# The upper weight sum of the projections' seven-product pairs, made by an adding transfer of GpSimd's queue instead of a VectorE addition

## The chip, the core and the metric

The kernel runs on one core of one Trainium2 chip. The metric is the device time of one execution in microseconds (us). Every run lists the time of the whole execution; the profiler adds the span from the first to the last instruction of one profiled execution. Engines are named as the profile names them: PE (TensorE matmuls), ACT (ScalarE), DVE (VectorE), POOL (GpSimd) and SP (SyncE, which here only issues transfers). An engine works through its instructions in the order in which they stand in its queue, and an instruction that waits holds back all that stand behind it on that engine.

## The reference

Two layers, each a mixer and a feed-forward part, on 256 tokens of 2048 columns in float32.

```python
for l in range(DEPTH):
    h = rms_norm(x, pre_mix_norm[l])
    m = hybrid_mixer(h, l, w_in[l], w_o[l], ...)      # h @ w_in, two kinds of attention, mix @ w_o
    x = x + rms_norm(m, post_mix_norm[l])
    h = rms_norm(x, pre_ffn_norm[l])
    f = swiglu(h, w_gate[l], w_up[l], w_down[l])      # (silu(h @ w_gate) * (h @ w_up)) @ w_down
    x = x + rms_norm(f, post_ffn_norm[l])
```

The change concerns the two projections of the mixer: `h @ w_in` (2048 to 6144 columns; its columns are the q, k and v of eight stick-breaking heads and of eight differential heads) and `mix @ w_o` (2048 to 2048).

## The kernel before

**Weights.** All weights are cut into blocks of 256 rows (two groups of 128 partitions) by 512 columns, 512 KB each, and laid out in the order of their use: 784 blocks, 392 a layer. `weight_order` makes the order; the number in a tile's name (`GU21`, `hi21`) is the block's place in it. A block `i` is loaded by SP (`fetch`, L258), then split into a rounded part `hi` (ACT) and a rest `lo` (DVE), both in float32r, and a product is three matmuls: left-hi by hi, left-hi by lo, left-lo by hi (`product`, L1225 to L1227). Weight blocks are prepared four ahead of the one in use (`LOOKAHEAD`), and the `hi` and `lo` tiles have six buffers each.

**Seven-product pairs.** Two weight blocks of the same rows and two column groups, g (block i-1) and u (block i), with the two token halves, make a two-by-two block product. Some of these pairs are done with seven products in place of eight. They need sums of weight blocks, which `mixed_weights(i)` makes from the loaded tiles g and u, whose halves `[:, 0, :]` and `[:, 1, :]` are the upper and the lower 128 rows:

- T1 = upper g + upper u, written over upper u. This is the sum that the change moves. `split(hi, lo, u)` then splits T1 and lower u together (ACT L307, DVE L309).
- T2 = lower u - T1 (DVE L318), then split into the third part of `Th`, `Tl`.
- g + T2 (DVE L319, both halves), which gives T3 and T4, then split into the first two parts of `Th`, `Tl`.

The matmuls of a pair (`seven_products`) come in this order: upper g (`hi`, `lo` of block i-1), lower g, T1, lower u, T2, T3, T4.

**Which pairs.** In the feed-forward part 122 pairs (`sevens`) have their own way: `summed` loads u into a tile T up to four blocks early and GpSimd's queue adds upper g onto it straight from the weights in memory (L275, `accum_op=ALU.add`). In the input projection there are ten pairs a layer and in the output projection four (`plain`, `own`): 28 in all. Their u is loaded like other blocks, into a tile GU (`late_room`, four buffers) or V (two buffers), and T1 is made by DVE at L313.

**The input projection around the change.** The columns are taken in six pairs of column groups (`PAIRS`). The first pair, (6, 8), has no seven-product pairs. When its sums are complete, `settle` scales them (ACT L1055, tiles `tok`), and `rotate` turns the first quarter of each head dimension by four small operations on POOL for each of four tiles (L914 to L917). Meanwhile the second column pair, (10, 7), starts; its third weight pair, blocks 20 and 21, is the first seven-product pair of the layer, blocks 24 and 25 the second. In layer 1 the same places are blocks 412, 413 and 416, 417. Each of the first column pairs is followed by the attention work of finished heads, which is spread between the matmuls.

**What sets the order.** The program is recorded in the order of the code, and a scheduler with its own estimates of durations then sets each engine's queue; `issue_after` puts one instruction behind another (`after_rests()` puts L313 behind the newest plain rest on DVE; `not_ahead` keeps a load of a pair behind earlier loads on SP), and `high_priority` moves work ahead. An instruction waits for the ones whose data it needs.

Of the kernel before, what the change touches and what calls it, by code (L numbers as in the profile page):

```python
# [13 lines left out]
ALU = mybir.AluOpType  # L14
# [170 lines left out]
def kernel(  # L185
# [15 lines left out]
    nc = tc.nc  # L201
# [19 lines left out]
    order, plan, sevens, plain, own, aside = weight_order()  # L221
    stream = [weights_in_turn[i].rearrange("p (k n) -> p k n", k=2) for i in range(len(order))]
# [12 lines left out]
    def fetch(upto):  # L235
        while len(raws) < min(upto, len(stream)):
            i = len(raws)
            for j in range(i, min(i + EARLY + 1, mix_raw[3])):
                if j in sevens and j not in sums:
                    summed(j)  # L240
            if i in sevens:
                raws.append(sums[i])
                continue
            if i + 1 in sevens:
                g = mix_raw[0].tile([P, 2, CW], F32, tag="G", bufs=mix_raw[1], name=f"G{i}")
                with not_ahead(i):
                    loads.append(nc.sync.dma_start(g, stream[i]))
                raws.append(g)
                continue
            if i in own or i + 1 in own:  # L250
                raw = mix_pool[0].tile([P, 2, CW], F32, tag="v", bufs=2, name=f"V{i}")
            elif i in plain or i + 1 in plain:
                raw = late_room([P, 2, CW], f"GU{i}")
            else:
                raw = wpool.tile([P, 2, CW], F32, tag="raw", bufs=4, name=f"raw{i}")
            mixing = bool({i, i + 1} & (own | plain))
            with not_ahead(i) if mixing else nullcontext():
                loads.append(nc.sync.dma_start(raw, stream[i]))  # L258
            raws.append(raw)
            if not mixing:  # L260
                usual.append((i, loads[-1]))

    usual = []

    def not_ahead(i):

        return tc.issue_after(next(load.ins for j, load in reversed(usual) if j <= i - LEAD))

    sums = {}
    def summed(i):  # L270

        sums[i] = mix_raw[0].tile([P, 2, CW], F32, tag="T", bufs=mix_raw[2], name=f"T{i}")
        with not_ahead(i):
            loads.append(nc.sync.dma_start(sums[i], stream[i]))
        nc.gpsimd.dma_start(sums[i][:, 0, :], stream[i - 1][:, 0, :], accum_op=ALU.add)  # L275
# [5 lines left out]
    def mixed_weights(i):  # L281

        g, u = raws[i - 1], raws[i]
        hi = wpool.tile([P, 2, CW], F32R, tag="hi", bufs=6, name=f"hi{i}")
        lo = wpool.tile([P, 2, CW], F32R, tag="lo", bufs=6, name=f"lo{i}")
        if i in own or i in aside:
            th = wpool.tile([P, 2, CW], F32R, tag="hi", bufs=6, name=f"Th{i}")
            tl = wpool.tile([P, 2, CW], F32R, tag="lo", bufs=6, name=f"Tl{i}")
        if i in own:
            th2 = mix_pool[0].tile([P, 2 * (S + P)], F32R, tag="ah", bufs=1, name=f"T2h{i}")[:, 0:CW]  # L290
            tl2 = mix_pool[0].tile([P, 2 * (S + P)], F32R, tag="al", bufs=1, name=f"T2l{i}")[:, 0:CW]
        elif i in aside:
            if aside[i] == "v":
                both = heads_pool[0].tile([P, 2, CW], F32R, tag="v", bufs=2, name=f"T2{i}")
                th2, tl2 = both[:, 0, :], both[:, 1, :]
            else:
                th2, tl2 = (
                    mix_pool[0].tile([P, 4, P], F32R, tag=tag, bufs=len(IN_SEVEN), name=f"T2{tag}{i}").rearrange("p j c -> p (j c)")
                    for tag in ("sh", "sl")
                )  # L300
        else:
            th = mix_pool[0].tile([P, 3, CW], F32R, tag="Th", bufs=1 if i in plain else 2, name=f"Th{i}")
            tl = mix_pool[0].tile([P, 3, CW], F32R, tag="Tl", bufs=1 if i in plain else 2, name=f"Tl{i}")
            th2, tl2 = th[:, 2, :], tl[:, 2, :]

        def split(h, l, w):
            nc.scalar.activation(h, w, AF.Copy)  # L307
            with in_row(i):
                newest_rest[i] = nc.vector.tensor_tensor(out=l, in0=w, in1=h.bitcast(F32), op=ALU.subtract)  # L309

        if i in plain or i in own:
            with after_rests():
                nc.vector.tensor_tensor(out=u[:, 0, :], in0=g[:, 0, :], in1=u[:, 0, :], op=ALU.add)  # L313
        split(hi, lo, u)
        t1, b22 = ((hi[:, k, :], lo[:, k, :]) for k in range(2))
        t3, t4 = ((th[:, k, :], tl[:, k, :]) for k in range(2))
        t2 = u[:, 1, :]
        nc.vector.tensor_tensor(out=t2, in0=t2, in1=u[:, 0, :], op=ALU.subtract)  # L318
        nc.vector.tensor_tensor(out=g, in0=g, in1=t2.unsqueeze(1).to_broadcast([P, 2, CW]), op=ALU.add)  # L319
        split(th2, tl2, t2)  # L320
        split(th[:, 0:2, :], tl[:, 0:2, :], g)
        t2 = th2, tl2
        return {"b22": b22, "t1": t1, "t2": t2, "t3": t3, "t4": t4}

    def feed(upto):
        fetch(upto)
        while fed[0] < min(upto, len(stream)):
            i = fed[0]
            raw = raws[i]
            if i in sevens or i in plain or i in own:  # L330
                ready[i] = mixed_weights(i)
                fed[0] += 1
                continue
            hi = wpool.tile([P, 2, CW], F32R, tag="hi", bufs=6, name=f"hi{i}")
            nc.scalar.activation(hi, raw, AF.Copy)  # L335
            lo = wpool.tile([P, 2, CW], F32R, tag="lo", bufs=6, name=f"lo{i}")
            if i in helped:
                rest = nc.gpsimd.tensor_tensor(out=lo, in0=raw, in1=hi.bitcast(F32), op=ALU.subtract)
                if helped[i]:
                    tc.add_manual_dep(rest.ins, newest_seven[0].ins.name, AFTER, reason="the shared port")  # L340
                ready[i] = (hi, lo)
                fed[0] += 1
                continue
            with behind():
                rest = nc.vector.tensor_tensor(out=lo, in0=raw, in1=hi.bitcast(F32), op=ALU.subtract)  # L345
            ready[i] = (hi, lo)
            fed[0] += 1
            rests.append(rest)

    def rounded_next():  # L350

        i = fed[0]
        fetch(i + 1)
        raw = raws[i]
        hi = wpool.tile([P, 2, CW], F32R, tag="hi", bufs=6, name=f"hi{i}")
        nc.scalar.activation(hi, raw, AF.Copy)
        lo = wpool.tile([P, 2, CW], F32R, tag="lo", bufs=6, name=f"lo{i}")
        ready[i] = (hi, lo)
        fed[0] += 1

        def rest(eng=nc.vector):
            r = eng.tensor_tensor(out=lo, in0=raw, in1=hi.bitcast(F32), op=ALU.subtract)
            if eng is nc.vector:
                rests.append(r)
            return r

        return rest
# [5 lines left out]
    def in_row(i):  # L373

        return tc.issue_after(follows[i].ins) if i in follows else nullcontext()
# [8 lines left out]
    def after_rests():  # L384

        return tc.issue_after(rests[-1].ins)
# [39 lines left out]
    def late_room(shape, name, dtype=F32):  # L426

        return rooms.tile(shape, dtype, tag="late", name=name)
# [490 lines left out]
    def opening(pool, accs, xT, stats, sums_of, settle):  # L919
# [33 lines left out]
        for kk in range(2):  # L953
            for i in range(2):
                loads.append(nc.sync.dma_start(raws[i][:, kk, :], stream[i][:, kk, :]))
        load()
        fetch(4)
        for kk in range(2):
            split(kk)
# [407 lines left out]
    for l in range(L):  # L1367
# [42 lines left out]
        for kp in LATE_O[:-1]:  # L1410
            i, j = (plan[l]["o"][c, kp] for c in (2, 3))
# [97 lines left out]
        for c in range(FF // CW):  # L1509
# [47 lines left out]
            for t in range(NT):  # L1557
                nc.vector.scalar_tensor_tensor(
                    out=results[c][t], in0=banks[2 * t + 1], scalar=rs[t][:, 0:1], in1=w[2 * t], op0=ALU.mult, op1=ALU.mult
# [197 lines left out]
```

## Time and profile before

| what | value |
|---|---|
| three runs | 2177.02 us median, 2175.26 to 2178.78 |
| the profiled execution's own time | 2176.12 us |
| its span, first to last instruction | 2174.4 us, TensorE clock granted 0.999 |
| ACT busy | 1415.4 us (65%) |
| POOL busy | 246.4 us (11%) |
| transfers | 470.44 MB, mean 216 GB/s |
| GpSimd's queue | 17600 packets, 32.02 MB, 8.9% of 16 transfer engines' span |

Matmuls are pipelined, so PE's busy time says only that it always has one under way; where it waits is read from the view of waits. A row of the timeline has the start and the duration in us, the engine, the source line, the operation and its output and inputs without their numbers, the shapes, a count, and in brackets the idle time of the engine before it and what ended that.

### The profile page before, as it was taken

The page shows a single profiled execution, that of the slowest core. Times are in us where ns is not written, and L with a number is a line of the kernel's source. Part 1 is how long each engine was busy: PE and PEld are TensorE (multiplying, and loading weights), DVE is VectorE, ACT ScalarE, POOL GpSimd, SP SyncE. Part 2 cuts the span into 40 slices and gives each one's busy share as a digit, 9 for nine tenths or more (in the row PEclk, how much of TensorE's full clock was granted, in tenths as well). Part 3 has the DMA queues.
Part 4 walks back from the last instruction along what each step waited for, and adds up shares of the span by engine and source line. Part 5 has one row for each costly group of instructions (what it writes and reads, how often), then busy time and mean ns, then how long its engine had stood idle before and what let it go on. Part 6 is the DMA issues. An engine that isn't in the chain of part 4 may idle for free.

```text
span 2174.4 us, 28786 instructions
## 1 busy us (share of the span) xinstructions
PE 2162.2 (99%) x9932; PEld 1778.7 (82%) x9932; DVE 1959.8 (90%) x2705; ACT 1415.4 (65%) x2113; POOL 246.4 (11%) x239
## 2 busy tenths in 40 slices
PE   9999999999999999999999999999999999999998
PEld 7888888888888888888888888888888888888886
DVE  7888978899999999999878888779999999999997
ACT  7666775765666666666575667757566666676664
POOL 1100000022221220000010000000212222200000
PEclk9999999999999999999999999999999999999999
DMA  8545446497887876768465464455978878767683
GB/s 315 204 165 196 161 174 204 153 306 233 246 259 224 230 236 225 235 224 257 146 245 175 171 206 161 172 182 183 302 232 253 254 224 243 226 220 241 202 270 98
DMA packets 140275, 470.44 MB, mean 216 GB/s; under 512 B 15952, under 2 KB 16976, under 8 KB 139616
## 3 DMA queue, kind: packets, MB, share of 16 engines
q1 hardware_dynamic: 121952, 436.03, 58.3%
q0 software_dynamic: 17600, 32.02, 8.9%
q8 instruction: 78, 1.28, 0.2%
q10 hardware_dynamic: 576, 0.54, 0.1%
q14 instruction: 69, 0.57, 0.1%
HBM read 460.14 MB, written 8.39 MB: 215 GB/s over the span
## 4 chain that ended last, share of the span: by engine, by line
PE 90%; DVE 5%; issue 2%; ACT 1%; DMA 1%; DVEq 0%; ACTq 0%
PE c L1282 20%; PE in L1225 6%; PE in L1227 6%; PE in L1226 6%; PE dn L1608 4%; PE dn L1605 4%; PE dn L1606 4%; PE p L1226 3%; PE c L1225 2%; PE c L1227 2%; PE p L1227 2%; PE c L1226 2%; PE p L1225 2%; PE o L636 2%; PE o L634 2%; PE o L635 2%
## 5 line engine op out<-in xcount | busy, mean ns | idle before, releaser
L345 DVE TENSOR_TENSOR lo<-raw,hi 128x1024 fp32r<-128x1024 f32 x442 | 535.4, 1231 | 54.6 <-ACT hi L335 53.5
L335 ACT ACTIVATE hi<-raw 128x1024 fp32r<-128x1024 f32 x464 | 473.6, 1054 | 69.2 <-DMA raw<-in_weights_in_turn_dram 25.4
L1282 PE MATMUL c<-hi,xF 128*128 128x512 f32 x1344 | 364.5, 392 | 0.6 <-DVE xF L544 0.5
L1282 PEld LDWEIGHTS c<-hi,xF 128*128 128x128 f32 x1344 | 249.8, 188 | 53.3 <-ACT act L1492 1.7
L275 POOL DMA_DIRECT2D T<-in_weights_in_turn_dram x122 | 107.3, 879 | 1363.7 <-DVE f L1499 557.3
L1282 PE MATMUL c<-lo,xF 128*128 128x512 f32 x672 | 207.4, 390 | 0.0
L307 ACT ACTIVATE Th<-T 128x512 fp32r<-128x512 f32 x122 | 77.2, 633 | 196.6 <-DVE T L318 194.2
L307 ACT ACTIVATE Th<-G 128x1024 fp32r<-128x1024 f32 x122 | 129.1, 1058 | 79.3 <-DVE G L319 78.4
L1605 PE MATMUL dn<-hi,jh 128*128 128x512 f32 x416 | 162.0, 389 | 0.0
L1606 PE MATMUL dn<-lo,jh 128*128 128x512 f32 x416 | 161.8, 389 | 0.0
L309 DVE TENSOR_TENSOR Tl<-G,Th 128x1024 fp32r<-128x1024 f32 x122 | 149.1, 1222 | 11.6 <-ACT Th L307 11.6
L335 ACT ACTIVATE hi<-G 128x1024 fp32r<-128x1024 f32 x122 | 128.9, 1057 | 36.6 <-DMA G<-in_weights_in_turn_dram 18.4
L309 DVE TENSOR_TENSOR lo<-T,hi 128x1024 fp32r<-128x1024 f32 x122 | 151.3, 1240 | 0.1
L319 DVE TENSOR_TENSOR G<-G,T 128x1024 f32<-128x1024 f32 x122 | 148.9, 1221 | 2.6 <-DVE T L318 0.9
L1282 PEld LDWEIGHTS c<-lo,xF 128*128 128x128 f32 x672 | 126.0, 188 | 26.5
L345 DVE TENSOR_TENSOR lo<-G,hi 128x1024 fp32r<-128x1024 f32 x104 | 127.0, 1221 | 10.1 <-ACT hi L335 10.0
L307 ACT ACTIVATE hi<-T 128x1024 fp32r<-128x1024 f32 x122 | 128.1, 1050 | 11.5 <-PE c L1227 8.0
L1608 PE MATMUL dn<-hi,jl 128*128 128x512 f32 x416 | 128.1, 389 | 0.0
L1225 PE MATMUL in<-hi,xT 128*128 128x512 f32 x316 | 126.0, 400 | 0.4 <-ACT hi L961 0.4
L1226 PE MATMUL in<-lo,xT 128*128 128x512 f32 x316 | 123.3, 391 | 0.3 <-DVE lo L345 0.2
L1227 PE MATMUL in<-hi,xT 128*128 128x512 f32 x316 | 123.1, 391 | 0.0
L1225 PE MATMUL in<-hi,xI 128*128 128x512 f32 x292 | 117.1, 401 | 0.0
(532 smaller groups left out, 5049.4 us busy)
## 6 DMA issues: line engine op xcount, KB each, us to landing
raw<-in_weights_in_turn_dram SPq DMA_DIRECT2D x482, 512.0 KB, 4.8
T<-in_weights_in_turn_dram SPq DMA_DIRECT2D x122, 512.0 KB, 5.2
G<-in_weights_in_turn_dram SPq DMA_DIRECT2D x122, 512.0 KB, 5.4
T<-in_weights_in_turn_dram POOLq DMA_DIRECT2D x122, 256.0 KB, 5.6
GU<-in_weights_in_turn_dram SPq DMA_DIRECT2D x48, 512.0 KB, 6.2
V<-in_weights_in_turn_dram SPq DMA_DIRECT2D x8, 512.0 KB, 5.6
away_ffn<-x SPq DMA_DIRECT2D x8, 512.0 KB, 7.5
xd<-away_ffn SPq DMA_DIRECT2D x8, 512.0 KB, 9.0
```

Of the source, the lines that this page charges most:

```text
L307: nc.scalar.activation(h, w, AF.Copy)
L309: newest_rest[i] = nc.vector.tensor_tensor(out=l, in0=w, in1=h.bitcast(F32), op=ALU.subtract)
L319: nc.vector.tensor_tensor(out=g, in0=g, in1=t2.unsqueeze(1).to_broadcast([P, 2, CW]), op=ALU.add)
L335: nc.scalar.activation(hi, raw, AF.Copy)
L345: rest = nc.vector.tensor_tensor(out=lo, in0=raw, in1=hi.bitcast(F32), op=ALU.subtract)
L1225: nc.tensor.matmul(a, sh, hi, start=first, stop=False, skip_group_check=open_sums[0])
L1226: nc.tensor.matmul(a, sh, lo, start=False, stop=False, skip_group_check=open_sums[0])
L1227: return nc.tensor.matmul(a, sl, hi, start=False, stop=last, skip_group_check=open_sums[0])
L1282: nc.tensor.matmul(a, stat[part], w[j][:, kk, :], start=first and kk + n == 0, stop=last and kk == 1 and n == 2)
L1605: nc.tensor.matmul(accs[c, t], sh, hi[:, kk, :], start=first, stop=False, skip_group_check=open_sums[0])
L1606: nc.tensor.matmul(accs[c, t], sh, lo[:, kk, :], start=False, stop=False, skip_group_check=open_sums[0])
L1608: nc.tensor.matmul(accs[c, t], sl, hi[:, kk, :], start=False, stop=last, skip_group_check=open_sums[0])
```

## The change

The addition at L313 is taken out of `mixed_weights`. In `fetch`, right behind the load of a block u of the 28 pairs, GpSimd's queue gets a transfer that adds upper g, read from the weights in memory, onto upper u in its tile. The numbers are the same; the transfer waits for the load of u to land.

```diff
@@ fetch @@
             if not mixing:
                 usual.append((i, loads[-1]))
+            elif i in own or i in plain:
+                nc.gpsimd.dma_start(raw[:, 0, :], stream[i - 1][:, 0, :], accum_op=ALU.add)
@@ mixed_weights @@
-        if i in plain or i in own:
-            with after_rests():
-                nc.vector.tensor_tensor(out=u[:, 0, :], in0=g[:, 0, :], in1=u[:, 0, :], op=ALU.add)
         split(hi, lo, u)
```

The scheduler also places other instructions anew. Three places follow; the line numbers of the changed kernel are two higher below the first edit and one lower behind the second.

POOL of the changed kernel in layer 0, between the rotation of the last of the four tiles of column pair (6, 8) (`tok0_8_1`) and the first rotation of the next column pair (`tok0_7_0`):

```order
L913 TENSOR_TENSOR ra_0_8_1_582<-tok0_8_1_580,rope_sb_95 128x128
L914 TENSOR_TENSOR rb_0_8_1_583<-tok0_8_1_580,rope_sb_95 128x8x8
L915 TENSOR_TENSOR rb_0_8_1_583<-tok0_8_1_580,rope_sb_95 128x8x8
L916 TENSOR_TENSOR tok0_8_1_580<-ra_0_8_1_582,rb_0_8_1_583 128x8x16
L263 DMA GU21_622<-in_weights_in_turn_dram 128x512
L263 DMA GU25_712<-in_weights_in_turn_dram 128x512
L263 DMA GU37_1024<-in_weights_in_turn_dram 128x512
L263 DMA GU41_1146<-in_weights_in_turn_dram 128x512
L913 TENSOR_TENSOR ra_0_7_0_979<-tok0_7_0_977,rope_sb_95 128x128
```

Before, `ra_0_7_0` stood directly behind `tok0_8_1`; the four adding transfers are new, and the first stands behind all sixteen operations of the four rotations.

DVE in layer 0 around block 21 (`Tl21` first from T2, then from T3 and T4 together). Before:

```order
L345 TENSOR_TENSOR lo20_620<-GU20_600,hi20_618 128x1024
L313 TENSOR_TENSOR GU21_622<-GU20_600,GU21_622 128x512
L309 TENSOR_TENSOR lo21_625<-GU21_622,hi21_624 128x1024
L318 TENSOR_TENSOR GU21_622<-GU21_622 128x512
L345 TENSOR_TENSOR lo22_670<-raw22_666,hi22_668 128x1024
L319 TENSOR_TENSOR GU20_600<-GU20_600,GU21_622 128x1024
L309 TENSOR_TENSOR Tl21_627<-GU21_622,Th21_626 128x512
L345 TENSOR_TENSOR lo23_676<-raw23_672,hi23_674 128x1024
L309 TENSOR_TENSOR Tl21_627<-GU20_600,Th21_626 128x1024
```

and with the change:

```order
L344 TENSOR_TENSOR lo20_620<-GU20_600,hi20_618 128x1024
L311 TENSOR_TENSOR lo21_626<-GU21_622,hi21_625 128x1024
L344 TENSOR_TENSOR lo22_670<-raw22_666,hi22_668 128x1024
L317 TENSOR_TENSOR GU21_622<-GU21_622 128x512
L344 TENSOR_TENSOR lo23_676<-raw23_672,hi23_674 128x1024
L318 TENSOR_TENSOR GU20_600<-GU20_600,GU21_622 128x1024
L311 TENSOR_TENSOR Tl21_628<-GU21_622,Th21_627 128x512
L311 TENSOR_TENSOR Tl21_628<-GU20_600,Th21_627 128x1024
```

The addition is gone, and `lo22` and `lo23` now stand ahead of the steps that lead to T3 and T4. On ACT `hi21` stands directly behind `hi20` in both kernels, with `hi22` and `hi23` behind it.

POOL of the changed kernel in layer 1, at the same place of the program:

```order
L263 DMA GU413_10501<-in_weights_in_turn_dram 128x512
L913 TENSOR_TENSOR ra_1_6_0_10449<-tok1_6_0_10447,rope_sb_95 128x128
...
L916 TENSOR_TENSOR tok1_8_1_10483<-ra_1_8_1_10485,rb_1_8_1_10486 128x8x16
L263 DMA GU417_10586<-in_weights_in_turn_dram 128x512
L263 DMA GU429_10883<-in_weights_in_turn_dram 128x512
```

Here the first transfer (block 413) stands ahead of the four rotations, and the second (block 417) behind them.

## The prediction

> **What bounds the kernel now.** I read the busy times first, then the chain of waits, then what PE waited for in the two stretches where the change acts: the input and output projection with the attention, 40 to 385 us (layer 0) and 1105 to 1460 us (layer 1).
>
> ```profile
> PE 2162.2 (99%) x9932; PEld 1778.7 (82%) x9932; DVE 1959.8 (90%) x2705; ACT 1415.4 (65%) x2113; POOL 246.4 (11%) x239
> PE 90%; DVE 5%; issue 2%; ACT 1%; DMA 1%; DVEq 0%; ACTq 0%
> ```
>
> PE is 90% of the chain that ends last. The only wait of PE that the view lists in the two stretches is one in each, layer 0 first:
>
> ```profile
> PE pT_df L895 <- DVE w L1268: 0.2, 1, 0.2
> ```
> ```profile
> PE pT_df L895 <- DVE w L1268: 0.5, 1, 0.5
> ```
>
> So PE's stream sets the time here. Work taken off DVE can win back at most 0.2 + 0.5 = 0.7 us; anything that makes PE wait adds in full, since PE, busy for 99% of the span, has no idle time later in which to make it up.
>
> **What is removed.** The two groups of additions, and what ACT's idle time says of them:
>
> ```profile
> L313 DVE TENSOR_TENSOR GU<-GU,GU x24: 670/686/954, 53.9 to 1377.2; 128x512 f32<-128x512 f32 x24
> L313 DVE TENSOR_TENSOR V<-V,V x4: 681/685/686, 342.8 to 1441.5; 128x512 f32<-128x512 f32 x4
>   DVE GU L313: 27.9, 15
> ```
>
> 28 x 0.69 = 19.2 us of DVE time, and 27.9 us in which ACT stood idle for the sum before it could split u. Both lie beside PE's matmuls, so they are worth nothing by themselves. I take the 0.7 us of PE's two waits as won, because both are waits for DVE and two additions stand ahead of each; the other bound is 0.
>
> **What is added.** 28 adding transfers of 256 KB. The kernel has the same transfer 122 times in the feed-forward part:
>
> ```profile
> DMA to landing us min/median/max: 3.6/5.6/8.6
> ```
>
> From the start of the issue on POOL to the landing takes 5.6 us in the middle, 3.6 to 8.6 at the ends. The sum takes 0.69 us on DVE; as a transfer eight times as long. That matters where the loaded tile was there just in time, or where the transfer is issued late. For most blocks it is not so. Block 37 stands for 20 of the 28:
>
> ```profile
> 71.25 0.42 SPq L258 DMA_DIRECT2D GU<-in_weights_in_turn_dram  x1
> 100.94 1.06 ACT L307 ACTIVATE hi<-GU 128x1024 fp32r<-128x1024 f32 x1 [2.21 <-DVE GU L313]
> DMA to landing us min/median/max: 4.1/6.2/9.1
> ```
>
> Its load is issued 29.7 us before ACT wants the sum; the slowest load (9.1) and the slowest adding transfer (8.6) together take 17.7. Cost nothing; the cover is the early load, and without it each would cost what the next paragraphs work out.
>
> The V blocks are tighter. The last of layer 0, block 121 (load, split of u, last rest, and the matmul that reads it first):
>
> ```profile
> 350.20 1.52 SPq L258 DMA_DIRECT2D V<-in_weights_in_turn_dram  x2
> 360.22 1.06 ACT L307 ACTIVATE hi<-V 128x1024 fp32r<-128x1024 f32 x1 [2.24 <-DVE V L313]
> 365.74 1.23 DVE L309 TENSOR_TENSOR Tl<-V,Th 128x1024 fp32r<-128x1024 f32 x1 [0.61 <-ACT Th L307]
> 373.22 0.39 PE L1226 MATMUL p_o<-Tl,sho 128*128 128x512 f32 x1
> ```
>
> The second load is issued by 351.4; with the middle values 6.2 and 5.6 the sum lands at 363.2, 3.0 us late on ACT, and PE has 373.2 - 367.0 = 6.2 us in hand. Cost nothing.
>
> **Block 21, where it costs.** The first transfer stands on POOL behind four rotations. They run now as follows (POOL, then DVE at the same time):
>
> ```profile
> 48.44 0.46 POOL L914 TENSOR_TENSOR ra<-tok,rope_sb 128x128 f32<-128x128 f32 x1 [11.57 <-ACT tok L1055]
> ...
> 50.08 1.49 POOL L914 TENSOR_TENSOR ra<-tok,rope_sb 128x128 f32<-128x128 f32 x1
> ...
> 52.75 1.54 POOL L914 TENSOR_TENSOR ra<-tok,rope_sb 128x128 f32<-128x128 f32 x1
> ...
> 58.45 1.33 POOL L917 TENSOR_TENSOR tok<-ra,rb 128x128 f32<-128x128 f32 x1
> ```
> ```profile
> 52.74 1.23 DVE L345 TENSOR_TENSOR lo<-GU,hi 128x1024 fp32r<-128x1024 f32 x1 [1.50 <-ACT hi L335]
> ```
>
> They end at 59.8 us. The rotation's first operation takes 0.46 us alone and 1.54 beside a DVE subtraction, so DVE holds it up. In the changed order DVE has nothing to do behind lo20 (end 53.97) until block 21's sum has landed, so the rest runs undisturbed: the third `ra` ends at 54.29 as now, the rest of its rotation takes 1.2 us by the first rotation's starts (48.90 to 50.08), the fourth 50.08 - 48.44 = 1.6. POOL is free at 57.1 us, and the tile has long been loaded. The rule of the Trainium skill (SBUF — State Buffer, Who interferes with whom) is that a VectorE instruction with two SBUF inputs and a GpSimd instruction that reads SBUF exclude each other for a whole instruction. The trace agrees (1.54 against 0.46 us); if the stretching were something else and stayed, POOL would be free at 59.8 and the forecast would be 2.7 us higher.
>
> How long the transfer takes there depends on the traffic (the last two columns are the transfer engines' busy share and GB/s):
>
> ```profile
> 57.00:60.00 3.00, 3.00 (x15) 2.50 (x14) 2.97 (x4) 1.52 (x2) 2.71 (x3) 1.00 0.87 350
> 60.00:63.00 3.00, 3.00 (x15) 2.49 (x14) 3.00 (x4) 2.01 (x2) 0.00 (x0) 1.00 0.58 187
> ```
>
> Two weight loads are still under way, so not 3.6; but the next load waits for a tile that lo22 frees, and lo22 is now held up too, so not 8.6 either. I take 5.6: the sum is there at 57.1 + 5.6 = 62.7 us. From there ACT and DVE go on in the order of the change, with the durations of this pair's `Th` (ACT) and the next pair's rests (DVE), and block 37's `hi` above:
>
> ```profile
> 60.90 1.06 ACT L307 ACTIVATE Th<-GU 128x1024 fp32r<-128x1024 f32 x1 [2.04 <-DVE GU L319]
> ```
> ```profile
> 66.74 1.23 DVE L309 TENSOR_TENSOR lo<-GU,hi 128x1024 fp32r<-128x1024 f32 x1 [1.26 <-ACT hi L307]
> 67.88 1.22 DVE L345 TENSOR_TENSOR lo<-raw,hi 128x1024 fp32r<-128x1024 f32 x1
> 69.02 0.69 DVE L318 TENSOR_TENSOR GU<-GU 128x512 f32<-128x512 f32 x1
> ...
> 70.75 1.22 DVE L319 TENSOR_TENSOR GU<-GU,GU 128x1024 f32<-128x1024 f32 x1
> ...
> 73.10 1.23 DVE L309 TENSOR_TENSOR Tl<-GU,Th 128x1024 fp32r<-128x1024 f32 x1 [0.53 <-ACT Th L307]
> ```
>
> hi21 1.06, lo21 1.23, lo22 1.22, T2 0.69, lo23 1.22, g + T2 1.22, Th 1.06 (Tl of T2 beside it), Tl of T3 and T4 1.23: 8.9 us, and 9.0 with a little for the steps from engine to engine (an estimate). Tl21 is complete at 71.7. PE now reads T1 and the rest of T3 first at
>
> ```profile
> 63.11 0.39 PE L1225 MATMUL q_in<-hi,shin 128*128 128x512 f32 x1
> 65.37 0.39 PE L1226 MATMUL p_in<-Tl,shin 128*128 128x512 f32 x1
> ```
>
> so PE stands 71.7 - 65.4 = 6.3 us. With 3.6 and 8.6 it is 4.3 and 9.3. Behind the waiting hi21 on ACT stand hi22, hi23 and the Th of the same pair; behind lo21 on DVE stand their rests; on SP the load that waits for lo22's tile; all slide with PE. Blocks 24 and 25 come after: DVE is then as far behind as PE is, so no second wait there. The transfer for block 25 has the load of its own tile to wait for and lands before ACT, held up, comes to it.
>
> **Layer 1 and the rest.** The transfer of block 413 stands ahead of the rotations, so only 417 comes late (end of the rotations, split of u, last rest, matmul):
>
> ```profile
> 1139.27 1.32 POOL L917 TENSOR_TENSOR tok<-ra,rb 128x128 f32<-128x128 f32 x1
> ```
> ```profile
> 1146.46 1.06 ACT L307 ACTIVATE hi<-GU 128x1024 fp32r<-128x1024 f32 x1 [2.16 <-DVE GU L313]
> 1153.91 1.23 DVE L309 TENSOR_TENSOR Tl<-GU,Th 128x1024 fp32r<-128x1024 f32 x1 [0.53 <-ACT Th L307]
> 1157.49 0.39 PE L1226 MATMUL p_in<-Tl,shin 128*128 128x512 f32 x1
> ```
>
> 1140.6 + 5.6 = 1146.2, as early as ACT wants it, and 2.3 us in hand on PE: nothing, at 8.6 some 0.4. The other rotations stand behind transfers whose loads have landed by then. The scheduler's other moves (in the last column pair, PE's transposes `pT_df` some matmuls earlier, DVE's inputs to them later) I take as 0, with up to 0.5 us a layer. The traffic, 7 MB more on 470, is in the 5.6.
>
> Sum: 6.3 - 0.7 = +5.6 us, on the profiled execution's own 2176.1 us 2181.7. The median of the runs shown lies 0.9 higher, and I forecast for a median: **2182.6 us**.
>
> **The rivals.** *DVE is the bound after all.* If the stretch from 89 to 126 us, where the chain of waits runs through DVE, and its twin in layer 1 were set by DVE, the two additions in each would count: 4 x 0.69 = 2.8 us, 2173 to 2174; if block 21 is hidden and only PE's 0.7 us counts, 2176. It decides if the sum lands before 65.4 - 9.0 = 56.4, so the issue would have to come by 50.8. ACT's 27.9 idle us speak for it; PE's waits of 0.2 and 0.5 us and the four rotations ahead speak against it. 0.12.
>
> *A short landing.* At the shortest of the 122, block 21 costs 4.3 - 0.7 = 3.6 us: 2180.6, under what can be told from no change. DVE's idleness and few loads behind speak for it, the share of 0.87 against it. 0.10. The Trainium skill (DMA: Bandwidth & Descriptors, Anatomy of one DMA) gives about 2.0 us plus bytes at 436 GB/s for such a transfer, here 2.6 as an estimate; by it the time would be 3.0 us under my forecast. No row of the 122 is that short, so the trace does not agree.
>
> *A slow landing behind a slow POOL.* If the rotations still end at 59.8 and the transfer shares the engines with two loads and takes 8.6, PE stands 6.3 + 2.7 + 3.0 = 12.0 us, and layer 1 adds up to 1: 2188 to 2190. The share of 0.87 speaks for it, the idle DVE against it. 0.14.
>
> **How the numbers follow.** The forecast, one wait of PE of 4.5 to 9.3 us at block 21, has 0.64; its own range is 2180 to 2187 (with the 1 us of the moves). The whole range takes in the short landing and half of the slow one: 2178 to 2190. About 0.2%, 4.4 us, is what a measurement can tell from no change. Faster: 0.03, the part of the first rival with 2.8 us and more. Same: 0.09 of the first rival, 0.09 of the short landing and 0.05 of the forecast's low end, 0.23. Slower: 0.74.
>
> **What would show it.** A wait of PE of some 6 us shortly before 72 us, put down to DVE's Tl or to the transfer, and ACT idle some 8 us ahead of `hi<-GU` behind DMA; POOL's adding transfer of block 21 at 57 to 58 us, landing at 61 to 66; no such wait near 1150; PE's waits of 0.2 and 0.5 us gone; DVE busy some 19 us less. I am wrong if PE does not wait there, if the two traces part somewhere else, or if the difference is not there by 130 us.

## The result, and the profile after

| | us |
|---|---|
| before, median of ten runs | 2177.11 (2175.26 to 2178.78) |
| with the change, median of ten runs | 2183.64 (2180.99 to 2185.67) |
| ratio, 95% interval | 1.0030 (1.0021 to 1.0039) |
| the profiled execution with the change, its span | 2182.66, 2180.9 |

The changed kernel is slower by 6.5 us. The page of its profiled execution, busy times and the chain of waits:

```profile
PE 2163.9 (99%) x9932; PEld 1780.2 (82%) x9932; DVE 1942.5 (89%) x2677; ACT 1417.3 (65%) x2113; POOL 267.4 (12%) x267
PE 88%; DVE 5%; DMA 3%; issue 2%; ACT 1%; POOL 0%; DVEq 0%; ACTq 0%; SPq 0%; POOLq 0%
```

DVE does 28 instructions and 17.3 us less, and the kernel is slower all the same. In the chain PE has given 2% of the span to DMA. The waits of PE in the changed kernel, from 40 to 395 us and, behind the dots, from 1105 to 1480 us (total, times, longest):

```profile
PE p_in L1225 <- DVE Tl L311: 2.5, 2, 1.7
PE p_in L1224 <- ACT Th L309: 0.8, 1, 0.8
PE xT_ps L529 <- DVE x L673: 0.3, 1, 0.3
...
PE xT_ps L529 <- DVE x L673: 0.7, 1, 0.7
```

The two waits of `pT_df` are gone, as forecast. New are 3.3 us at `p_in`, the sums of a seven-product pair, and small waits for x in the transposes `xT_ps` at the end of each mixer (0.3 and 0.7 us), which the prediction did not have.

**Block 21.** The timeline of the changed kernel: POOL (third rotation's start, last operation of the fourth, the transfers of blocks 21 and 25), then ACT, DVE and PE.

```profile
52.58 1.54 POOL L913 TENSOR_TENSOR ra<-tok,rope_sb 128x128 f32<-128x128 f32 x1
...
56.38 0.46 POOL L916 TENSOR_TENSOR tok<-ra,rb 128x128 f32<-128x128 f32 x1
56.78 1.78 POOL L263 DMA_DIRECT2D GU<-in_weights_in_turn_dram  x2
```
```profile
60.47 1.06 ACT L309 ACTIVATE hi<-GU 128x1024 fp32r<-128x1024 f32 x1 [7.93 <-DMA GU<-in_weights_in_turn_dram]
```
```profile
67.92 1.23 DVE L311 TENSOR_TENSOR Tl<-GU,Th 128x1024 fp32r<-128x1024 f32 x1 [0.53 <-ACT Th L309]
```
```profile
65.24 0.51 PE L1224 MATMUL p_in<-Th,shin 128*128 128x512 f32 x1 [0.78 <-ACT Th L309]
67.45 0.50 PE L1225 MATMUL p_in<-Tl,shin 128*128 128x512 f32 x1 [1.71 <-DVE Tl L311]
...
69.20 0.50 PE L1225 MATMUL p_in<-Tl,shin 128*128 128x512 f32 x1 [0.76 <-DVE Tl L311]
...
70.04 0.63 PE L1225 MATMUL in<-Tl,xT 128*128 128x512 f32 x1
70.47 0.63 PE L1226 MATMUL in<-Th,xT 128*128 128x512 f32 x1
...
73.42 0.39 PE L1224 MATMUL in<-hi,xT 128*128 128x512 f32 x1
73.65 0.39 PE L1225 MATMUL in<-lo,xT 128*128 128x512 f32 x1
```

The issue comes at 56.78, behind the rotations, and ACT gets the sum 3.7 us later. The chain to the end of `Tl` takes 60.47 to 69.15, 8.7 us. PE stands three times, for `Th` and `Tl` of T2 and for `Tl` of T3, 3.25 us in all, and reads the first `Tl` of T3 at 69.20 where it did so at 65.37. The last rows show what the prediction had not thought of: behind the stall the matmuls start 0.43 us apart, against 0.23 before and after. The view by windows has the reason in the column PEclk, third from the right (the last two are the transfer engines' share and GB/s):

```profile
65.00:70.00 5.00, 2.29 (x7) 1.34 (x8) 4.47 (x5) 3.36 (x5) 0.00 (x0) 1.00 0.60 208
70.00:73.50 3.50, 3.50 (x10) 2.72 (x9) 3.50 (x5) 1.91 (x3) 0.00 (x0) 0.52 0.00 0
73.50:77.00 3.50, 3.50 (x17) 2.92 (x16) 2.98 (x4) 1.47 (x2) 0.00 (x0) 1.00 0.98 345
```

PE is busy for 2.29 of 5 us, and then the granted clock is a half for 3.4 us: ten matmuls, where seventeen run in the same time before and after.

**Block 121, the last V block of layer 0.** ACT of the changed kernel (split of u of block 121, then blocks 126 and 127), and for the last row its counterpart before:

```profile
368.59 1.06 ACT L309 ACTIVATE hi<-V 128x1024 fp32r<-128x1024 f32 x1 [5.70 <-DMA V<-in_weights_in_turn_dram]
...
379.67 1.07 ACT L334 ACTIVATE hi<-raw 128x1024 fp32r<-128x1024 f32 x1 [1.33 <-DMA raw<-in_weights_in_turn_dram]
381.82 1.06 ACT L334 ACTIVATE hi<-raw 128x1024 fp32r<-128x1024 f32 x1 [1.08 <-DMA raw<-in_weights_in_turn_dram]
```
```profile
374.55 1.06 ACT L335 ACTIVATE hi<-raw 128x1024 fp32r<-128x1024 f32 x1 [0.93 <-PE o L1227]
```

And PE at the same two matmuls, the first that reads block 124 and the first transposes of x for the feed-forward part, before and with the change:

```profile
377.07 0.39 PE L634 MATMUL o<-hi,mix_sb 128*128 128x512 f32 x1
...
386.60 0.60 PE L530 MATMUL xT_ps<-ident,x 128*128 128x128 f32 x4
```
```profile
381.98 0.39 PE L633 MATMUL o<-hi,mix_sb 128*128 128x512 f32 x1
...
391.99 0.55 PE L529 MATMUL xT_ps<-ident,x 128*128 128x128 f32 x3 [0.33 <-DVE x L673]
```

PE stands 4.91 us behind the run of before at the first and 5.39 at the second. In between ACT waited for the loads of blocks 126 and 127. The split of 127 is 381.82 - 374.55 = 7.27 us later than before, of which 4.91 is PE's own delay by then; it is 2.4 us late against PE.

**Where the 6.5 us of the span lie.** The start of the same matmul in the two traces, with the change less before, is -0.2 us at 46 us (the start of the program), +5.6 at 80, +4.9 at 380, +5.4 at 388, +5.1 at 1160, +4.2 at 1460, +5.2 at 1470, +6.5 at 1600 and +6.5 at the end. So: block 21 with the slow clock +5.7, the attention parts -0.7 and -0.9, the ends of the two mixers +0.5 and +0.95, and the rest, some 1.0 less the 0.2 of the start, in the feed-forward parts. There nothing was changed, and every other kernel below also lies 0.3 to 1.6 us later at 1600 than at 1550 (between the same matmuls), so the one profiled execution of before was probably a good one there.

### The profile page after: what moved, and what is told of

It is laid out like the page before. It is cut to its first block, busy times and chain, and to the rows that moved or that the text cites. A ratio compares the mean times of both kernels' runs of the same rounds, so it can differ in the third digit from the quotient of the medians.

```text
span 2180.9 us, 28869 instructions
## 1 busy us (share of the span) xinstructions
PE 2163.9 (99%) x9932; PEld 1780.2 (82%) x9932; DVE 1942.5 (89%) x2677; ACT 1417.3 (65%) x2113; POOL 267.4 (12%) x267
## 3 DMA queue, kind: packets, MB, share of 16 engines
q8 instruction: 78, 1.28, 0.2%
## 4 chain that ended last, share of the span: by engine, by line
PE 88%; DVE 5%; DMA 3%; issue 2%; ACT 1%; POOL 0%; DVEq 0%; ACTq 0%; SPq 0%; POOLq 0%
PE c L1281 20%; PE in L1224 6%; PE in L1226 6%; PE in L1225 6%; PE dn L1607 4%; PE dn L1605 4%; PE dn L1604 4%; PE p L1225 3%; PE p L1226 3%; PE c L1226 3%; PE c L1225 3%; PE c L1224 3%; PE p L1224 3%; DMA raw<-in_weights_in_turn_dram 1%; DVE lo L344 1%
```

## The experiments

Each expectation was written ahead of its run. Every run has its own runs of before on the same chip; medians and 95% intervals of the ratio:

| kernel | median | before | ratio |
|---|---|---|---|
| 27 transfers (block 21 on VectorE) | 2177.67 | 2178.00 | 0.9998 (0.9989 to 1.0007) |
| block 21 alone | 2184.53 | 2178.00 | 1.0031 (1.0020 to 1.0043) |
| 28, block 21 ahead of the rotations | 2181.24 | 2178.00 | 1.0012 (1.0004 to 1.0021) |
| 28, PE's waits filled | 2183.79 | 2178.00 | 1.0028 (1.0019 to 1.0038) |
| 23 (block 21 and V on VectorE) | 2174.57 | 2177.14 | 0.9988 (0.9980 to 0.9997) |
| 24 (V on VectorE) | 2181.65 | 2177.14 | 1.0020 (1.0010 to 1.0029) |
| V alone | 2181.93 | 2177.14 | 1.0023 (1.0013 to 1.0033) |
| 24, PE's waits filled | 2179.02 | 2177.14 | 1.0011 (1.0002 to 1.0020) |
| 27, splits of the next blocks first | 2175.16 | 2176.50 | 0.9994 (0.9985 to 1.0003) |

And from their profiled executions, what PE lost (or won) in each stretch against the run of before, as the start of the same matmuls at the end of the stretch less that at its beginning, in us. Each row is one execution. Those of runs 2, 6 and 7 (block 21 alone, 24, V alone) lie 3.3, 2.5 and 2.8 us above the medians of their kernels, the others within 1.5 us:

| kernel | 46 to 80, block 21 | 80 to 380 | 380 to 388, end of mixer 0 | 1160 to 1460 | 1460 to 1470, end of mixer 1 |
|---|---|---|---|---|---|
| the change | +5.7 | -0.7 | +0.5 | -0.9 | +0.95 |
| 27 | 0.0 | -0.7 | +1.4 | -1.0 | 0.0 |
| block 21 alone | +6.45 | 0.0 | 0.0 | 0.0 | 0.0 |
| ahead of the rotations | +1.5 | -0.6 | +1.3 | -0.9 | +1.7 |
| 28 filled | +4.6 | -0.7 | +2.9 | -0.8 | +1.7 |
| 23 | 0.0 | -0.7 | 0.0 | -0.9 | 0.0 |
| 24 | +8.2 | -0.7 | 0.0 | -0.9 | 0.0 |
| V alone | 0.0 | 0.0 | +2.1 | +0.6 | +3.35 |
| 24 filled | +5.05 | -0.7 | 0.0 | -0.9 | 0.0 |
| 27, next splits first | 0.0 | -0.6 | 0.0 | -0.9 | 0.0 |

**1. All but block 21.** In all kernels with fewer transfers, the blocks in a set `BY_DVE` keep the addition (shown once):

```diff
+    BY_DVE = {21}
@@ fetch @@
-            elif i in own or i in plain:
+            elif (i in own or i in plain) and i not in BY_DVE:
                 nc.gpsimd.dma_start(raw[:, 0, :], stream[i - 1][:, 0, :], accum_op=ALU.add)
@@ mixed_weights @@
+        if i in BY_DVE:
+            with after_rests():
+                nc.vector.tensor_tensor(out=u[:, 0, :], in0=g[:, 0, :], in1=u[:, 0, :], op=ALU.add)
         split(hi, lo, u)
```

> All as in the change, but the sum of block 21 stays an addition of VectorE: 27 transfers. Theory (the whole loss is block 21's late sum, and the half clock that follows the stall): no wait of PE near 65 us, clock 1.00 from 65 to 75 us, time 2175.5 to 2177.5, that is no loss against before. Rival (the transfers cost in general, by their traffic, GpSimd's queue or the moved order): time stays at 2182 to 2184.

No wait near 65 us, a clock of 1.00, and 2177.67, just above the range expected: 0.9998 of before. The loss of 6.5 us is gone, which rules out a general cost of the transfers of that size. But PE waits at the end of the first mixer, and longer than in the change:

```profile
PE xT_ps L533 <- DVE x L677: 1.2, 1, 1.2
```

**2. Block 21 alone** (`BY_DVE` holds the other 27).

> Only block 21's sum is made by a transfer, the other 27 are VectorE additions. Theory: PE stands some 4 us between 65 and 70 us, the clock falls to about a half for some 3.4 us behind it, +5.6 us by 80 us and 2182 to 2183.5 at the end; the transfer lands 3.6 to 5.6 us behind its issue near 57 us. Rival (the transfers in general): a loss of no more than 1 us, 2177 to 2178.

2184.53, 1.0031 of before and 1 us above the range expected: the full loss from one transfer of 28. It is issued at 57.91, ACT starts at 61.71, and PE loses 6.45 us by 80 us, 1.6 of them behind the stall, at half the clock. The theory of block 21 holds; nothing is lost or won anywhere else in the mixers. This execution is longer than the run of before by another 5 us, which lie at the start (1.0) and in the feed-forward parts.

**3. Block 21's transfer ahead of the rotations.** The four rotations are recorded behind it on GpSimd; no other engine's order changes.

```diff
@@ fetch @@
-                nc.gpsimd.dma_start(raw[:, 0, :], stream[i - 1][:, 0, :], accum_op=ALU.add)
+                added = nc.gpsimd.dma_start(raw[:, 0, :], stream[i - 1][:, 0, :], accum_op=ALU.add)
+                while i == 21 and later:
+                    rotate(*later.pop(0), added)
@@ rotate, which gets an argument behind=None; later begins as an empty list @@
+        if behind is None and nm in ("0_6_0", "0_8_0", "0_6_1", "0_8_1"):
+            later.append((pool, tok, t, nm))
+            return
...
+        with tc.issue_after(behind.ins) if behind else nullcontext():
             eng.tensor_tensor(out=ra, in0=v16, in1=table(0, 16), op=ALU.mult)
```

> All 28 transfers, but in layer 0 the transfer of block 21 stands ahead of the four rotations on GpSimd's queue; the order of the other engines is the same. Theory (the place behind the rotations sets the landing): the transfer is issued when its tile's load has landed, some 53 to 55 us, lands at 57 to 60, Tl21 follows 8.7 us later at 66 to 69, so PE waits 1 to 3 us less than in the change and the clock falls less or not at all: 2177 to 2180.5. Rival (the transfer's own duration, not its place): 2182 to 2184. Second rival (the rotations, now later, hold up the attention): a new wait of PE on tok behind 80 us.

POOL issues it 6.7 us earlier than in the change, at 50.05 and not between 53 and 55 as expected, yet ACT gets the sum only 1.4 us earlier:

```profile
50.05 0.88 POOL L263 DMA_DIRECT2D GU<-in_weights_in_turn_dram  x1
```
```profile
59.08 1.06 ACT L311 ACTIVATE hi<-GU 128x1024 fp32r<-128x1024 f32 x1 [5.31 <-DMA GU<-in_weights_in_turn_dram]
```

It takes 9.0 us here and 3.7 in the change. The windows from issue to landing, the change first:

```profile
56.80:60.40 3.60, 3.60 (x17) 2.99 (x16) 0.00 (x0) 0.00 (x0) 1.77 (x3) 1.00 0.69 142
```
```profile
50.00:59.00 9.00, 9.00 (x42) 7.44 (x41) 2.65 (x2) 3.37 (x5) 8.08 (x16) 1.00 0.98 353
```

Early, it runs beside the weight loads at a share of 0.98, and its first packet starts 4.1 us behind the issue; late, the loads are nearly through, and the first packet starts after 1.6 us. So the place behind the rotations is only part of the delay. These are times from the start of the program, and PE's matmuls lie 1.24 us later in this execution from 46 us on (+1.07 against -0.17). Against PE the issue is 8.0 us earlier and the sum 2.6 us. These 2.6 us took PE's three waits down to one of 0.8 us and kept the clock at 1.00, and PE's loss falls from 5.7 to 1.5 us: 2.6 us less standing and the 1.6 us of the slow clock. The wait on `tok` that the second rival expected does not come. The total of 2181.24 is above what I expected; in the traced execution both mixer ends cost more (1.3 and 1.7 us).

**4. PE's waits filled.** Fourteen matmuls, overwritten by the first product that starts the sum `p7` anew:

```diff
             if n % 2 == 0:
                 tick()
+            if m is ready.get(21):
+                for _ in range({4: 10, 5: 4}.get(n, 0)):
+                    nc.tensor.matmul(p7, a22[0], m["b22" if n == 4 else "t2"][0], start=True, stop=True)
             newest_seven[0] = product(*job)
```

> All 28 transfers as in the change, and 14 matmuls whose result is overwritten stand on PE where it waits for block 21, 10 ahead of T2's product and 4 ahead of T3's: about 3.2 us of PE time, as long as the waits. Theory (the slow matmuls from 70 to 73.4 us come from PE's idleness ahead of them): Tl21 is read at about the same time, 69.2 us, the clock stays 1.00 from 70 to 75 us, and the end comes some 1.6 us earlier than in the change, 2181.5 to 2182.5. Rival (the pace has another cause, such as the work of the other engines just then): the matmuls stay at 0.43 us apart for 3.4 us, time 2183.6 or a little more.

The clock stays at 1.00 throughout and the matmuls behind the stall run at full pace, though the transfer lands 0.5 us later than in the change (60.84 - 56.66 = 4.2 us). So PE's idleness is the cause of the slow pace, and the rival is out. But the median did not fall: 2183.79, 1.0028 of before against 1.0030 for the change. In the traced execution (2182.30) the ends of the mixers took 2.9 and 1.7 us and hid the gain; whether they do so in the median is not shown here. That, and the same wait in runs 1 and 3 and never in run 2, turned the question to the V blocks.

**5. Neither block 21 nor V** (`BY_DVE = own | {21}`).

> The sums of block 21 and of the four V blocks (115, 121, 507, 513) stay VectorE additions: 23 transfers. Theory (block 21 costs some 5.7 us, and each layer's last V block, whose sum lands 7 to 9 us behind its issue, holds back the raw loads behind it and costs 0 to 2.9 us at the layer's last transposes): no wait of PE on x in the transposes xT_ps behind 380 and 1460 us beyond 0.3 us; against the traced run of before the matmuls run some 0.8 us earlier by 380 us and some 1.7 by 1460 us, and that stays; time 1 to 2 us under the run with 27 transfers, 2175.5 to 2177, a little faster than before. Rival (the waits on x have to do with the other transfers or with chance): they are there as in the run with 27 transfers, and the time is the same as that run's.

2174.57, 1 us below the range expected and 0.9988 of before, with the interval below 1: **faster than both kernels**. No wait on x at either mixer's end. The attention parts keep their -0.7 and -0.9 us, more than the two waits of `pT_df`.

**6. V alone left to VectorE** (`BY_DVE = own`).

> The sums of the four V blocks alone stay VectorE additions: 24 transfers, block 21's among them. Theory: block 21's stall and the half clock as in the change, no wait on x at the ends of the two mixers, 1.5 to 2.5 us under the change: 2181 to 2182.5. Rival (no cost of the V blocks): 2183.6, with waits of 0.5 to 1.6 us on x.

2181.65, as expected: the ends of the mixers are free, block 21 costs all it did. In the traced execution the half clock lasts twice as long as in that of the change:

```profile
69.00:70.00 1.00, 0.33 (x2) 0.02 (x1) 1.00 (x2) 1.00 (x2) 0.00 (x0) 0.62 0.63 246
70.00:75.00 5.00, 4.91 (x12) 3.84 (x13) 5.00 (x6) 3.21 (x4) 0.00 (x0) 0.50 0.13 22
75.00:76.00 1.00, 1.00 (x4) 0.81 (x3) 1.00 (x2) 0.00 (x0) 0.00 (x0) 0.50 0.93 365
76.00:77.00 1.00, 1.00 (x6) 0.83 (x5) 0.92 (x2) 0.65 (x1) 0.00 (x0) 0.96 1.06 414
```

**7. V alone by transfers** (`BY_DVE = plain`).

> The four V blocks alone are summed by transfers, the other 24 by VectorE. Theory: nothing at 65 us; PE waits on x in the transposes xT_ps at the end of one mixer or of both, by 0.5 to 2 us each, in step with how late hi of block 127 and 519 is made, by more than some 1.8 us: 0.5 to 3.5 us over before, 2178.5 to 2181. Rival (no cost of the V blocks): the same as before, no such wait.

2181.93, 1.0023 of before, 0.9 us above the range expected: four transfers that I had put at nothing cost 4.8 us when they stand alone. The waits at the ends of both mixers, layer 0 first, and one more in layer 1:

```profile
PE xT_ps L533 <- DVE x L677: 1.6, 1, 1.6
...
PE xT_ps L533 <- DVE x L677: 1.6, 1, 1.6
PE p_o L1229 <- DVE Tl L312: 0.3, 1, 0.3
```

The split of V is late by 4.6 us (block 121) and 6.6 us (513), against PE. The 6.6 us are over the 6.2 us that the prediction gave PE in hand for `Tl`, and here PE does wait for it, at 1458 us; with the next matmuls it loses 0.5 us there, most of the +0.6 in the table above. Over the kernels with V transfers PE's loss at the mixer's end follows the lateness of the split of block 127 (519 in layer 1), worked out as for the change above:

| lateness of the split, us | 1.76 | 2.36 | 2.78 | 3.12 | 3.22 | 3.52 | 3.56 | 3.96 | 4.74 | 5.19 |
|---|---|---|---|---|---|---|---|---|---|---|
| PE's loss at the mixer's end, us | 0.0 | 0.52 | 0.95 | 1.28 | 1.39 | 1.70 | 1.73 | 2.13 | 2.91 | 3.35 |

From 2.36 on it is the lateness less 1.83 us, to 0.02: that split has 1.83 us in hand, and what comes over it is lost in full. (The last column is layer 1 of this run, counted from behind the wait for `Tl`.)

**8. V on VectorE, PE's waits filled** (run 6 with the edit of run 4).

> As the run with 24 transfers, and the 14 overwritten matmuls stand where PE waits for block 21. With the V blocks out of the way the two differ by the fill alone. Theory (the clock falls because PE stands idle): clock 1.00 from 65 to 77 us, and 1.2 to 1.7 us under the run with 24 transfers. Rival (the fill costs elsewhere what the clock gives): the same time as that run.

2179.02, 2.6 us under run 6 on the same chip; the intervals of the two ratios overlap (1.0002 to 1.0020 and 1.0010 to 1.0029), so the size is rough. The clock is 1.00 all through:

```profile
65.00:70.00 5.00, 4.31 (x19) 3.26 (x18) 4.48 (x6) 2.44 (x3) 0.00 (x0) 1.00 0.63 200
70.00:73.50 3.50, 3.50 (x17) 2.67 (x16) 3.50 (x4) 3.05 (x4) 0.00 (x0) 1.00 0.04 14
```

The gain is larger than the 1.2 to 1.7 us expected; in the traced execution of run 6 the clock was low for two spans of 3.4 us, worth 2.15 us (PE's loss since 46 us goes from 6.0 to 8.2 us behind the stall).

**9. The next blocks' splits ahead of V's.** Run 1 with the two raw blocks behind block 121, and behind 513 (`last_sums` holds the two numbers), split first; DVE and ACT change their order at these two places and nothing else moves.

```diff
@@ feed, whose splitting of one block is now prepare(i) @@
+            if i in last_sums:
+                fetch(i + 3)
+                for j in (i + 1, i + 2, i):
+                    prepare(j)
+            elif i not in ready:
+                prepare(i)
             fed[0] += 1
```

> As the run with 27 transfers (block 21's sum on VectorE, the four V blocks' sums by transfers), and in both layers the splits of the two raw blocks behind the last V block (122 and 123, 514 and 515) stand ahead of that block's own splits on ScalarE and VectorE. Nothing else moves, and the sum of block 121 lands as late as in that run. Theory (the V block's late sum costs nothing by itself, PE having 6 us in hand for its products, but it holds the splits behind it, those hold the raw tiles, and the loads of blocks 126 and 127 come late): the loads of 126 and 518 are issued earlier than before by several us, no wait on x in xT_ps at the mixers' ends, 2174 to 2175.5, like the run with 23 transfers. Rival (the late sum delays the pair's own products or the last sums directly): waits on x as in the run with 27 transfers, 0.5 to 2 us, and 2177 to 2178. Second rival (the splits of 121, now two places later, become late themselves): a wait of PE on Tl of block 121 near 372 us.

The split of u of block 121 begins 4.2 us late against before, as late as in run 1, and nothing follows from it:

```profile
358.55 1.06 ACT L347 ACTIVATE hi<-raw 128x1024 fp32r<-128x1024 f32 x1 [0.98 <-PE o L1237]
361.22 1.06 ACT L347 ACTIVATE hi<-raw 128x1024 fp32r<-128x1024 f32 x1 [1.61 <-PE o L646]
363.99 1.06 ACT L311 ACTIVATE hi<-V 128x1024 fp32r<-128x1024 f32 x1 [1.71 <-PE o L646]
```

Blocks 122 and 123 are split in the time in which ACT waited for V, their raw tiles come free, the load of 126 is issued 6.8 us earlier than before, and the splits of 126 and 127 stand where they stood. No wait on x, none on `Tl`; 2175.16, within the range expected, 0.9994 of before, where the interval still holds 1. By the medians this run can't be told from run 1 (0.9998); it is the traces that show the loss of 1.4 us at the mixer's end gone. So a split of V that is 4.2 us late costs nothing by itself; what it holds up on ACT and DVE costs.

## Why the prediction was right, and where it was not

*What bounds the kernel.* Right: PE's stream. 17 us of DVE's time are gone and the attention parts win 1.6 us.

*Won.* Taken as 0.7 us, and called the most that could be won; measured 1.6 (0.7 and 0.9, the same in all kernels with the 20 early blocks by transfer). At PE's two waits on `w` the offset falls by 0.3 and 0.6 us; the rest lies between 240 and 310 and between 1320 and 1390 us, in steps of about 0.1 us, too small for the view of waits, and was not followed further. So the bound taken from that view was too low.

*Twenty blocks at nothing.* Right: run 5 has them all and loses nowhere in the mixers.

*Block 21: the mechanism.* Right in each link: transfer behind the rotations, rotations undisturbed once DVE has nothing to do, POOL free at 56.8 (57.1 forecast), the chain of 8.7 us (9.0), PE standing for the sums of block 21, no second wait at block 25. The one wait that was forecast, at T3, came as three, the first two already at T2. Runs 1 and 2 show that this is the loss.

*Block 21: the size.* The term of the sum that was mis-sized is the landing: 5.6 us taken, 3.7 measured. I had counted two loads under way. They had been issued 1.7 and 0.2 us earlier than before (48.58 and 51.10 against 50.25 and 51.27) and were nearly through: from 57 to 60 us the weight loads brought 44 packets of 4 KB, against 256 before. With DVE and ACT standing no new one came until 63.95 (before: 59.49). In the other kernels with the transfer at this place it took 3.8 to 4.9 us. So PE's standing cost 4.15 us by the offset at 66 us, and not 6.3. The Trainium skill (DMA: Bandwidth & Descriptors, Anatomy of one DMA) would have it at 2.6, an estimate; nothing here came under 3.6, though the landing at low traffic came nearer to it than I had thought.

*Block 21: the missing term.* The prediction had no price for what a stall does to PE's clock. It was 1.6 us in the change, by the offsets at 66 and 80 us, and in the comparison of runs 6 and 8 filling the wait was worth 2.6. With it block 21 costs 5.7 us, close to the 6.3 forecast: two errors of about 2 us in opposite directions. That the forecast for block 21 came so near is luck.

*V blocks at nothing.* This step failed. It asked whether PE would wait for `Tl` of block 121, which has 6.2 us in hand; the split came 3.5 us late (3.0 forecast), and PE did not wait. It did not ask what is queued behind `hi121` and `lo121`: the splits of 122 and 123, whose raw tiles the loads of 126 and 127 wait for, and the split of block 127 has 1.83 us in hand. The cost is 1.5 us in the traced execution of the change, and by medians 2.2: from run 5 to run 1 and from run 6 to the change the ratio rises by 0.0010 each. In run 7, without the other transfers, it is 4.8 by the median and 6.0 in the traced execution; why the sums come later there was not followed.

*Layer 1 at block 417.* Right, no wait there in any kernel. *Reorders at nothing.* Right as far as a loss goes.

*The sum.* By medians: the 23 harmless transfers -2.6 us (run 5), block 21 +7.0 (from run 5 to run 6), V +2.2 (from run 6 to the change): +6.6. These are steps on one way from before to the change, so they add up to the loss measured by the way they were taken; the check is that run 1, on the other way, gives the same +2.2 for V and +7.0 for block 21 (each of the ratios is known to 0.0009, some 2 us). The forecast of +5.6 had +6.3 for block 21, 0 for V and -0.7 for the rest. It came within 1 us of the loss measured because these errors, too, partly cancel.

*The rivals.* DVE as the bound: no, the sum lands at 60.4, not before 56.4. The short landing: true as to the landing, but its total of 2180.6 left out the clock and V. The slow landing behind a slow POOL: POOL was not slow; slow landings came where the transfer was issued early (run 3) and for V.

## What to carry to other kernels

When an operation gets more latency, ask of each instruction queued behind its consumer what it frees and who waits for that: V's products had 6 us to spare, the loads two steps behind had 1.8. A short stall of TensorE can be dearer than it looks, because the clock can fall behind it; work that is thrown away kept it up here (run 8: 2.6 us won, run 4: nothing by the median). Count an edit site by site: 23 of the 28 together won 2.6 us, one cost 7 and four cost 2, and leaving these five out turned a loss of 0.30% into a gain of 0.12%.

## What the runs showed of the hardware that was not expected

The granted TensorE clock fell to 0.50 behind three short waits (0.78, 1.71 and 0.76 us with four matmuls between the first and the last) in 4.7 us, and came back after 3.4 us of slow work. In run 6 it stayed low for 6.8 us, twice that: the shares of 0.62 and 0.96 in the windows of 1 us put the half clock from 69.2 to 76.1. Run 2 shows 6.8 us as well, behind two waits of 0.9 and 1.7 us. One wait of 0.8 us (run 3) and two of 0.7 and 0.4 (run 8) left it at 1.00. In the 3.4 us ahead of the fall PE was busy for 1.75 us in the change, 1.40 in run 6 and 1.22 in run 2. In the 3.4 us behind it PE was busy throughout in the change, and the clock came back at their end; in runs 6 and 2 it still stood for 0.8 and 0.5 us in them, and the clock came back one such stretch later, all of it busy. The Trainium skill (TensorE: Matmul & The Clock Gate, What's actually happening) says that the array's clock is halved after an idle window of about 3.4 us and is whole again after a busy one, in windows that run freely; the lengths of 3.4 and 6.8 us agree with that. That the window has to be idle throughout does not: no gap here was longer than 1.72 us.

An adding transfer of 256 KB took 3.7 us from issue to the reader's start at 142 GB/s of other and own traffic and 9.0 us at 353 GB/s. In the quiet stretch the transfer engines were busy for 0.69 of the time at those 142 GB/s, where the plain loads of the change reach 345 GB/s at 0.98: per byte an adding transfer occupies them longer. The packets of the change show by how much: one of 2 KB takes 178 ns in the median when it adds and 84 ns in a plain load, and one of 4 KB in a plain load 159 ns.
